# A hybrid attention and mLSTM layer: two loads asked for earlier and an output-gate tile laid across a stage border

## The chip, the cores and the metric

The kernel runs on one core of a Trainium2 chip. The metric is the device time of one execution in microseconds. Before the change it was 2285.49 us, the median of three runs (2283.78 to 2286.15).

The engines are named as in the profile: PE does matrix products and transposes, DVE, ACT and POOL work element by element, SP issues nearly all DMA transfers and does nothing else. Each engine runs its own list of instructions in order and waits on semaphores for the others. An instruction that waits holds up all that stand behind it on its engine.

## The reference

One encoder layer over 2048 positions of width 1024, with batch 1. A conditioning vector gives shifts, scales and gates. Then, in short:

```
hmix = rms_norm(x, g_norm1) * (1 + scale1) + shift1
q_a, k_a, v_a, q_m, k_m, v_m, o_m, gates = split(hmix @ w_in)
att  = rms_norm(banded_attention(q_a, k_a, v_a, sink), g_attn_out)
q_m, k_m = split(silu(centred_dwconv(concat(q_m, k_m))))
h_m  = rms_norm(mlstm(forward) + mlstm(backward), g_mlstm_out)
h_m  = sigmoid(o_m) * h_m
x    = x + gate1 * (concat(att, h_m) @ w_out)
ff   = silu(gte) * up      # gte, up = split(norm2(x) @ w_ffn_in)
x    = x + gate2 * (ff @ w_ffn_out);  out = rms_norm(x, g_final)
```

Attention has 8 heads of 64 with 2 key heads and sees 128 positions to each side. The mLSTM has 4 heads of 128, worked in 16 chunks of 128 positions; each direction carries a state from chunk to chunk. The output gate is the sigmoid of o_m, computed as a tanh.

## The kernel before

**Stages.** The first stage normalises x, keeps its transpose hT on the chip as four blocks of 512 positions, and computes the columns of w_in that are wanted position by position. The second stage (up to about 580 us) computes the mLSTM. The third (to about 800 us) is attention. A tail follows in which the operands of the output projection are made, then the output projection (from 827 us), and from about 1002 us the feed-forward part. The products of the output projection and of the feed-forward part are arranged so that 7 products of half size do the work of 8, so weights are added and subtracted first; w_out's are prepared in stage two (`w_out_ops`) and stored to `wo_d`.

**Filler.** Stages two and three have chains of small work on DVE, ACT and POOL between the products on PE. To keep PE busy, a queue of generators, `fill`, holds the projections of w_in's remaining columns. Each `pull(n)` issues n of their matmuls (128x512, line 498, tile `gps`). A tile of 512 positions is 24 matmuls and a column group of 128 is four such tiles, 96 matmuls. `conv_tile` makes the mLSTM's queries and keys, `qk_att` those of attention, `o_tiles` the output gate (ACT's tanh into `oth`, then a store to `og_d`). A call of `beat` counts one step of a list of things to do later (`put_soon`), so that, say, a store is issued some pulls after its tile. `next_cols` hands out the weights of a column group and starts loading the next group of the list `coming`: a load into the single buffer `wraw`, a rounded copy on ACT (`whi`), and four differences on POOL (`wlo`).

**The backward pass of a head** goes through chunks 15 to 1. For each it transposes the key chunk on PE (line 612, `ktp`), makes a weighted value and a product, and accumulates the state on DVE (line 660, `cb`). Key and value blocks of 512 positions are loaded by `load_qk` and `load_v`, issued on SP in the order of the program. The key and query blocks share four buffers `mqk`. The first query block of the forward pass is asked for at chunk 2:

```
            if cc == 2:
                q_first = load_qk(h, 0, 0)
```

The forward pass multiplies keys and queries (line 679, `sps`), and at the end of each block `store` transposes the scaled result `hst` (line 735, `htp`) and stores it to `mxm_d`.

**Head 0** is prepared while w_out's generator still runs: a loop of 252 steps, one `pull` each, steps w_out's preparation and the gates. The last key block of head 0 is loaded at step 150, the second (`last[NB - 2]`) behind the loop. w_out's last stores are issued at step 242.

**The border.** After the last head the four column groups of attention's keys and first queries are drawn to their end, and then the pools of stage two are closed and those of stage three opened. Up to there the order on all engines is the program's. Behind it, until the tail, PE's order is still the program's, and the order on DVE, ACT, POOL and SP is set by a planner that weighs costs of its own. Stage three loads `skb`, builds the distance bias on POOL and DVE (`iota`, two selections, eight tiles `abias`), and starts with the last query group as its filler, then the output gates of head 0, head 1, and of heads 2 and 3 block by block (`lasts`).

**Attention** goes in 34 steps over 32 units. A step scores one unit (line 782, `as`, tiles `aq`, `ak`, `av` loaded two units ahead), normalises it on POOL (line 798), transposes the unit before (line 805, `atp`) and multiplies the one before that (`ao`). Each step makes ten pulls: one behind each of four scores, one behind the normalisation, one and two and two behind the transposes.

**The tail** loads the prepared w_out (`start_wo`, line 1037) into the buffers of hT blocks that no filler needs any more, splits it on ACT and DVE (`finish_wo`), and draws the rest of `fill`.

Of the kernel before, what the change touches and what calls it, by code (L numbers as in the profile page):

```python
# [21 lines left out]
P = 128  # L22
# [4 lines left out]
NB = T // 512  # L27
# [5 lines left out]
C_QA, C_KA, C_VA, C_QM, C_KM, C_VM, C_OM, C_G = 0, 512, 640, 768, 1280, 1792, 2304, 2816  # L33
# [3 lines left out]
def hybrid_layer_kernel(  # L37
# [14 lines left out]
    def bank(tag, name):  # L52
        return pp.tile([P, 512], F32, tag=tag, name=name, bufs={"g": 2, "a": 2, "b": 1, "c": 2, "d": 1}[tag])
# [55 lines left out]
    fill = deque()  # L109
    soon = []  # L110

    def put_soon(k, f, *args):

        soon.append([k, f, args])

    def beat(k=1):
        for e in soon:
            e[0] -= k
        due = [e for e in soon if e[0] <= 0]
        soon[:] = [e for e in soon if e[0] > 0]  # L120
        for _, f, args in sorted(due, key=lambda e: e[0]):
            f(*args)

    def pull(n=1):

        while n > 0:
            if not fill:
                n -= 1
                beat()
            elif next(fill[0], None) is None:  # L130
                fill.popleft()
            else:
                n -= 1
                beat()

    def finish_fill(g):
        while any(f is g for f in fill):
            pull()
# [102 lines left out]
    def cols_steps(c0):  # L241

        pl, i = wslots[0]
        wslots.rotate(-1)
        r = pl.tile([P, D], F32, tag="wraw", name="wraw", bufs=1)
        v = lambda t: t.rearrange("p (a b) -> p a b", a=KT)
        sp.dma_start(v(r), w_in[:, c0:c0 + P].rearrange("(k p) c -> p k c", p=P))
        yield None
        hi = pl.tile([P, D], F32R, tag=f"w{i}h", name="whi", bufs=1)
        lo = pl.tile([P, D], F32R, tag=f"w{i}l", name="wlo", bufs=1)  # L250
        act.activation(hi, r, AF.Copy)
        for u in range(4):
            q = slice(u * 256, (u + 1) * 256)
            pool.tensor_tensor(lo[:, q], r[:, q], hi[:, q].bitcast(F32), SUB)
            yield v(hi), v(lo)

    def proj_cols(c0):
        *_, w = cols_steps(c0)
        return w

    ready, coming = deque(), deque()

    def next_cols():

        w = ready.popleft()
        if coming and not ready:
            g = cols_steps(coming.popleft())
            put_soon(6, next, g)
            for u in range(3):
                put_soon(40 + 5 * u, next, g)  # L270
            put_soon(55, lambda: ready.append(next(g)))
        return w
# [5 lines left out]
    with tc.tile_pool(name="sw", bufs=2, side="right", reuse_waits="tile") as sw:  # L278
# [29 lines left out]
        def columns_of(z, o, n):  # L308
# [7 lines left out]
                           fill=NEG, base=0, channel_multiplier=-1)  # L316
        pool.affine_select(maskb[:, 1, :], maskb[:, 1, :], pattern=[[-1, P]], compare_op=ALU.is_ge,
                           fill=NEG, base=0, channel_multiplier=1)
# [125 lines left out]
        for n in range(NB):  # L444
# [13 lines left out]
            for i in range(4):  # L458
# [9 lines left out]
                if tt == 8:  # L468
# [3 lines left out]
                    wp = ctx.enter_context(tc.tile_pool(name="w", bufs=1, side="left", reuse_waits="tile"))  # L472
# [22 lines left out]
    def proj_mm(ps, w, n):  # L495
        for k in range(KT):
            for i in range(3):
                pe.matmul(ps, w[i == 2][:, k, :], hT[n](i == 1, k), start=(k == 0 and i == 0),  # L498
                          stop=(k == KT - 1 and i == 2))
                yield True  # L500
# [56 lines left out]
    oslots = deque()  # L557

    def o_tiles(heads, blocks, ws_):

        if not ws_:
            ws_.extend(proj_cols(C_OM + h * P) for h in heads)
        for n in blocks:
            for h, w in zip(heads, ws_):
                ps = bank("g", "gps")
                yield from proj_mm(ps, w, n)
                pl, tag = oslots[0]
                oslots.rotate(-1)
                t = pl.tile([P, 512], F32, tag=tag, name="oth", bufs=1)
                act.activation(t, ps, AF.Tanh, scale=0.5)  # L570
                sp.dma_start(og_d[4 * n:4 * n + 4, h].rearrange("c p t -> p c t"), t.rearrange("p (c t) -> p c t", c=4))

    later = []

    def tick():

        due = [f for k, f in later if k <= 0]
        later[:] = [[k - 1, f] for k, f in later if k > 0]
        for f in due:
            f()  # L580

    def load_v(h, n):
        va = s2.tile([P, 4, 129], F32, tag="mv", name="mv", bufs=2)
        sp.dma_start(va, vaug_d[n * 512:(n + 1) * 512, h, :].rearrange("(c p) d -> p c d", p=P))
        return va

    def load_qk(h, j, n):
        t = s2.tile([P, 512], F32, tag="mqk", name="mqk", bufs=4)
        sp.dma_start(t, qk_d[j, h, n])
        return t  # L590

    def load_last(h):
        return {NB - 1: (load_qk(h, 1, NB - 1), load_v(h, NB - 1))}

    def mlstm(h, nb, nf, last):
# [5 lines left out]
        def load_bc(cc):  # L601
            bc = s2.tile([P, 4, P], F32, tag="bc", name="bc", bufs=3)
            sp.dma_start(bc.rearrange("p j t -> p (j t)"), bc_d[h, cc].rearrange("j t -> (j t)").partition_broadcast(P))
            return bc
# [15 lines left out]
        def kv_mm(kn, vw, tag="a"):  # L620
            kvp = bank(tag, "kvp")
            pe.matmul(kvp[:, :129], kn, vw, start=True, stop=True)
            return kvp
# [17 lines left out]
        for cc in list(range(NT - 1, 0, -1)) + [0, 0, 0]:  # L641
            tick()
            n, i = divmod(cc, 4)
            if i == 3 and n and n - 1 not in blk:
                blk[n - 1] = (load_qk(h, 1, n - 1), load_v(h, n - 1))
            if cc == 2:
                q_first = load_qk(h, 0, 0)
            if cc in (6, 4, 2):
                bcs[3 - cc // 2] = load_bc(3 - cc // 2)
            if cc:  # L650
                todo.append((cc, *k_chunk(blk[n][0][:, i * P:(i + 1) * P], blk[n][1][:, i, :], 1, cc)))
                pull(nb - nb // 2)
            if len(todo) > 2 or (todo and not cc):
                c_, kn, vw = todo.popleft()
                kvp = kv_mm(kn, vw, "bcdc"[c_ % len("bcdc")])
                if c_ == NT - 1:
                    dve.tensor_copy(cb[:, c_ - 1, :], kvp[:, :129])
                else:
                    rr = row(1, c_)
                    dve.scalar_tensor_tensor(cb[:, c_ - 1, :], cb[:, c_, :], dec[:, rr:rr + 1], kvp[:, :129], MUL, ADD)  # L660
                pull(nb // 2)
# [79 lines left out]
        for cc in range(NT + 1):  # L741
            tick()
            if cc == NT - 3 and h + 1 < HM:
                last = load_last(h + 1)
# [227 lines left out]
    ready.extend((w_first, w_second))  # L972
    convs = [[conv_tile(j, h) for j in (1, 0)] for h in range(HM)]
    coming.extend(c0 + h * P for h in range(1, HM) for c0 in (C_KM, C_QM))
    coming.extend(C_QA + j * P for j in (4, 0, 1, 2, 3))
    for h in range(HM):
        fill.extend(convs[h])
    for i in range(2 * 96 + 60):
        for j, g in enumerate(steps):
            while due[j] <= i:  # L980
                due[j] = next(g)
        if i == 150:
            t = s2.tile([P, 512], F32, tag="og", name="mqk", bufs=1)
            sp.dma_start(t, qk_d[1, 0, NB - 1])
            last = {NB - 1: (t, load_v(0, NB - 1))}
        pull(1)
    assert min(due) > 1 << 20
    last[NB - 2] = load_qk(0, 1, NB - 2), load_v(0, NB - 2)
    tags2 = (("cacc", 4), ("ctanh", 2))
    first = [qk_att(s2, tags2, j) for j in (4, 0, 1, 2)]  # L990
    fill.extend(first)
    for h in range(HM):
        if h:
            for g in convs[h]:
                finish_fill(g)
        last = mlstm(h, 3, 11, last)
# [5 lines left out]
    while soon:  # L1002
        beat()
    win.close()
    assert not fill and not later
    s2s.close()
    s3s, mxs = ExitStack(), ExitStack()
    s3 = s3s.enter_context(tc.tile_pool(name="s3", bufs=2, side="right", reuse_waits="tile"))
# [17 lines left out]
    TO = [4 * n + i for n in BO for i in range(4)]  # L1026
    wo23 = []
    lasts = [o_tiles((2, 3), (n,), wo23) for n in BO]
    fill.extend([o_tiles((h,), range(NB), []) for h in (0, 1)] + lasts)
    oslots.append((wp, "oth"))  # L1030
    wo = []

    def start_wo(u):
# [120 lines left out]
    for s_ in range(len(order) + 2):  # L1154
        if s_ + 2 == NT:
            for g in second:
                finish_fill(g)
            beat(1 << 20)
        u0 = None
        if s_ < len(order):  # L1160
            u0 = Unit(*ahead.popleft())
        for g in range(4):
            if u0:
                u0.score(g)
            pull(1)
            if u2 and g < 3:
                u2.values(g)
        if s_ + 2 < len(order):
            ahead.append(att_loads(*order[s_ + 2]))
        if u0:  # L1170
            u0.normalize()
        pull(1)
        for i in range(3):
            if u1:
                u1.transpose(i)
            pull(1 if i == 0 else 2)
        u2, u1 = u1, u0
        if s_ > 20:
            next(chain0, None)
# [772 lines left out]
```

## Time and profile before

| | |
|---|---|
| runs | 2283.78, 2285.49, 2286.15 us |
| profiled execution, span | 2283.0 us (the page gives no other time for it) |
| PE / DVE / ACT / POOL busy | 97% / 71% / 46% / 47% of the span |
| mean granted PE clock | 0.995 |
| DMA | 391.28 MB, mean 171 GB/s |

The span runs from the first instruction to the last; the time of a run has some more around it. In the list of waits a row names the waiting engine, its instruction, the one that released it, and then the microseconds in total, how often, and the longest. In a timeline a row has its start, its length, the engine (SPq for a DMA issue), the line of the kernel, the operation, the tiles, the count, and in brackets the idle time before it and what ended that. Matmuls are pipelined, so the length of one is more than the distance to the next. In the view by windows the columns are the stretch, its length, the busy time of PE, PE's weight loads, DVE, ACT and POOL, the granted clock, the share of DMA and GB/s.

### The profile page before, as it was taken

To read this page: it belongs to the slowest core of one execution; us is meant where nothing else is said; L and a number is where in the kernel's file an instruction comes from. 1 tells how busy PE (TensorE), PEld (TensorE's weight loads), DVE (VectorE), ACT (ScalarE), POOL (GpSimd) and SP (SyncE) were. 2 spreads that over 40 slices of the span, in tenths; PEclk is the share of its full clock that TensorE was granted. 3 is DMA by queue.
4 is the path that set the end of the run, shared out by engine and by line. 5 is a ranking of instruction groups with operands and counts; after the bars stand their busy time and mean duration, and the time that the engine had idled before them with its cause. 6 is when DMAs were issued, how large, how long until landed. Compare 5 with 4: busy or idle time off the path is not lost.

```text
span 2283.0 us, 32447 instructions
## 1 busy us (share of the span) xinstructions
PE 2224.0 (97%) x10822; PEld 1859.5 (81%) x10822; DVE 1610.1 (71%) x2931; ACT 1058.6 (46%) x2206; POOL 1069.3 (47%) x927
## 2 busy tenths in 40 slices
PE   6999999999999999999999999999999999999998
PEld 4997788888788878788888888788888888888887
DVE  6787577656687887786756776666766666785594
ACT  5433565644577755344444444433333333233352
POOL 1006535334333434536656665566666654592020
PEclk9999999999999999999999999999999999999999
DMA  8476755676666576764353453533333374542462
GB/s 331 157 242 213 238 152 172 186 229 191 194 179 186 177 234 218 267 221 134 111 171 111 152 180 134 178 108 108 100 106 103 105 255 147 162 155 93 140 220 92
DMA packets 352811, 391.28 MB, mean 171 GB/s; under 512 B 21260, under 2 KB 251004, under 8 KB 352644
## 3 DMA queue, kind: packets, MB, share of 16 engines
q1 hardware_dynamic: 352420, 389.18, 52.5%
q8 instruction: 85, 1.39, 0.2%
q14 instruction: 82, 0.67, 0.1%
q10 hardware_dynamic: 224, 0.04, 0.0%
HBM read 269.95 MB, written 119.19 MB: 170 GB/s over the span
## 4 chain that ended last, share of the span: by engine, by line
PE 51%; DVE 3%; DMA 1%; issue 1%; ACT 1%; POOL 1%; SPq 0%; ACTq 0%; POOLq 0%; DVEq 0%
PE fp L56 11%; PE fp L57 11%; PE fp L58 11%; PE fo L58 5%; PE fo L57 5%; PE fo L56 5%; PE ops L56 1%; PE ops L57 1%; DMA al<-a_d 1%; PE ops L58 1%; DVE w L1721 1%; DVE al L1712 1%; DVE ra L1851 1%; PE trn L183 0%; DMA T<-hop_d 0%
## 5 line engine op out<-in xcount | busy, mean ns | idle before, releaser
L498 PE MATMUL gps<-hT,whi 128*128 128x512 f32 x1088 | 397.3, 420 | 0.3 <-DVE cacc L513 0.3
L57 PE MATMUL fo<-w,ah 128*128 128x512 f32 x616 | 239.8, 389 | 1.1 <-DVE w L1721 1.1
L58 PE MATMUL fo<-w,al 128*128 128x512 f32 x616 | 239.8, 389 | 0.5 <-DVE al L1712 0.5
L56 PE MATMUL fo<-w,ah 128*128 128x512 f32 x616 | 239.7, 389 | 0.0
L498 PE MATMUL gps<-hT,wlo 128*128 128x512 f32 x544 | 226.9, 417 | 0.0
L498 PEld LDWEIGHTS gps<-hT,whi 128*128 128x128 f32 x1088 | 200.5, 191 | 24.5 <-DVE cacc L513 0.7
L56 PE MATMUL fp<-T,S 128*128 128x512 f32 x528 | 206.9, 392 | 1.9 <-ACT s L1608 1.9
L57 PE MATMUL fp<-T,S 128*128 128x512 f32 x528 | 205.6, 389 | 0.0
L58 PE MATMUL fp<-T,S 128*128 128x512 f32 x528 | 205.4, 389 | 0.0
L1712 DVE TENSOR_TENSOR al<-al,ah 128x1024 fp32r<-128x1024 f32 x77 | 119.3, 1552 | 109.2 <-ACT ah L1711 109.0
L1711 ACT ACTIVATE ah<-al 128x1024 fp32r<-128x1024 f32 x77 | 81.6, 1060 | 188.5 <-DMA al<-a_d 186.9
L1451 DVE TENSOR_TENSOR S<-sf,S 128x512 fp32r<-128x512 f32 x86 | 130.4, 1554 | 37.4 <-ACT S L1450 37.2
L1451 DVE TENSOR_TENSOR A<-graw,A 128x512 fp32r<-128x512 f32 x86 | 128.4, 1515 | 16.3 <-ACT A L1450 16.3
L58 PE MATMUL fp<-B,A 128*128 128x512 f32 x352 | 136.9, 389 | 0.0
L56 PE MATMUL fp<-B,A 128*128 128x512 f32 x352 | 136.9, 389 | 0.0
L57 PE MATMUL fp<-B,A 128*128 128x512 f32 x352 | 136.9, 389 | 0.0
L57 PEld LDWEIGHTS fo<-w,ah 128*128 128x128 f32 x616 | 115.6, 188 | 25.6 <-DVE w L1721 1.6
L58 PEld LDWEIGHTS fo<-w,al 128*128 128x128 f32 x616 | 115.6, 188 | 24.9 <-DVE al L1712 1.0
L56 PEld LDWEIGHTS fo<-w,ah 128*128 128x128 f32 x616 | 115.6, 188 | 24.3 <-ACT ah L1711 0.2
L1616 DVE SCALAR_TENSOR_TENSOR g<-t,g 128x512 f32<-128x512 f32 x44 | 41.3, 939 | 132.2 <-ACT t L1615 132.2
L1455 POOL TENSOR_TENSOR sf<-A,A22r 128x512 f32<-128x512 f32 x43 | 61.0, 1419 | 154.9 <-DMA A22r<-in_w_ffn_in_dram 130.8
L798 POOL TENSOR_SCALAR ap<-ap,adn 128x384 f32<-128x384 f32 (+1 forms) x128 | 73.0, 590 | 129.2 <-DVE adn L796 71.7
(418 smaller groups left out, 6166.8 us busy)
## 6 DMA issues: line engine op xcount, KB each, us to landing
al<-a_d SPq DMA_DIRECT2D x77, 512.0 KB, 3.8
wmod<-in_w_mod_dram SPq DMA_DIRECT2D x48, 512.0 KB, 7.3
graw<-in_w_ffn_in_dram SPq DMA_DIRECT2D x43, 512.0 KB, 4.0
a_d<-ka SPq DMA_DIRECT2D x66, 256.0 KB, 4.6
bc<-bc_d SPq DMA_DIRECT2D x64, 256.0 KB, 3.7
hop_d<-n SPq DMA_DIRECT2D x56, 256.0 KB, 4.5
a_d<-u SPq DMA_DIRECT2D x55, 256.0 KB, 4.8
mqk<-qk_d SPq DMA_DIRECT2D x44, 256.0 KB, 4.0
```

What stands on the lines that cost most here:

```text
L56: pe.matmul(o, lh, rh, start=first, stop=False, skip_group_check=skip)
L57: pe.matmul(o, lh, rl, start=False, stop=False, skip_group_check=skip)
L58: pe.matmul(o, ll, rh, start=False, stop=last, skip_group_check=skip)
L498: pe.matmul(ps, w[i == 2][:, k, :], hT[n](i == 1, k), start=(k == 0 and i == 0), stop=(k == KT - 1 and i == 2))
L798: pool.tensor_scalar(self.p[g][:, :self.NK], self.p[g][:, :self.NK], dn[:, g:g + 1], 0.0, MUL, ADD)
L1451: dve.tensor_tensor(t[:, 1, :], f, t[:, 0, :].bitcast(F32), SUB)
L1455: pool.tensor_tensor(f1, a21, a22, ADD)
L1616: dve.scalar_tensor_tensor(g0, t0, 1.0, g0, ADD, MUL)
L1711: act.activation(ah, al.bitcast(F32), AF.Copy)
L1712: dve.tensor_tensor(al, al.bitcast(F32), ah.bitcast(F32), SUB)
L1721: dve.tensor_tensor(w[:, 1, :], f, w[:, 0, :].bitcast(F32), SUB)
L1851: dve.tensor_tensor(ra[i], ra[i], xr, ADD)
```

## The change

Three things are changed.

1. In each backward pass the first query block is asked for at chunk 6.
2. The second key block of head 0 and its values are asked for at step 222 of the loop, so their loads stand on SP ahead of w_out's last six stores.
3. The output gate of head 0 becomes a filler of its own, `o_first`, at the end of stage two's queue. Its weights are handed out by `next_cols`, so those of the last query group are loaded behind them. It is begun in stage two and finished in stage three. In exchange one pull is left out in every second step of attention.

```
-            if cc == 2:
+            if cc == 6:
                 q_first = load_qk(h, 0, 0)
...
-    coming.extend(C_QA + j * P for j in (4, 0, 1, 2, 3))
+    coming.extend(C_QA + j * P for j in (4, 0, 1, 2))
+    coming.extend((C_OM, C_QA + 3 * P))
...
+        if i == 222:
+            last[NB - 2] = load_qk(0, 1, NB - 2), load_v(0, NB - 2)
         pull(1)
     assert min(due) > 1 << 20
-    last[NB - 2] = load_qk(0, 1, NB - 2), load_v(0, NB - 2)
...
     fill.extend(first)
+
+    def o_first():
+        yield from o_tiles((0,), range(NB), [next_cols()])
+
+    fill.append(o_first())
+    oslots.append((wp, "oth"))
...
-    assert not fill and not later
+    assert len(fill) == 1 and not later
...
-    fill.extend([o_tiles((h,), range(NB), []) for h in (0, 1)] + lasts)
-    oslots.append((wp, "oth"))
+    fill.extend([o_tiles((1,), range(NB), [])] + lasts)
...
-            pull(1 if i == 0 else 2)
+            pull(1 if i == 0 or i == 2 and s_ % 2 else 2)
```

## The prediction

> **What bounds the kernel now.** I read the page's busy shares first, then the list of waits for PE, then the timeline around each wait that the change touches.
>
> ```profile
> PE 2224.0 (97%) x10822; PEld 1859.5 (81%) x10822; DVE 1610.1 (71%) x2931; ACT 1058.6 (46%) x2206; POOL 1069.3 (47%) x927
> ```
>
> PE is busy 97% of the 2283.0 us span, so only its idle time (59 us) and its pace can change. The list of waits says which idle time this change aims at (total, times, longest):
>
> ```profile
> PE htp L735 <- POOL hst L730: 5.6, 1, 5.6
> PE sps L679 <- DMA mqk<-qk_d: 3.2, 2, 1.7
> ...
> PE ktp L612 <- DMA mqk<-qk_d: 2.0, 1, 2.0
> ...
> PE sps L679 <- DVE cb L660: 1.1, 1, 1.1
> ```
>
> The first is the border between the mLSTM stage and the attention stage, the second the first query block of two heads, the third the second key block of head 0. The border costs more than its wait. The view by windows gives the granted clock in its sixth column of numbers, the timeline the pace:
>
> ```profile
> 574.20:579.60 5.40, 0.00 (x0) 0.00 (x0) 3.87 (x15) 1.34 (x6) 3.46 (x6) 0.91 0.41 103
> 579.60:585.30 5.70, 5.63 (x16) 4.57 (x17) 1.19 (x3) 0.69 (x1) 1.43 (x4) 0.50 0.62 198
> ```
>
> ```profile
> 579.67 1.12 PE L735 MATMUL htp<-ident,hst 128*128 128x128 f32 x4 [5.64 <-POOL hst L730]
> 580.44 1.20 PE L498 MATMUL gps<-hT,whi 128*128 128x512 f32 x2
> ...
> 588.10 0.39 PE L498 MATMUL gps<-hT,wlo 128*128 128x512 f32 x1
> 588.33 0.62 PE L498 MATMUL gps<-hT,whi 128*128 128x512 f32 x2
> 588.78 0.39 PE L498 MATMUL gps<-hT,wlo 128*128 128x512 f32 x1
> ...
> 591.06 0.28 PE L782 MATMUL as<-ak,aq 128*128 128x256 f32 x1
> ```
>
> Three matmuls take 0.68 us at full clock (588.10 to 588.78), 0.227 each. After 5.4 us without a matmul the clock is 0.50 for 5.7 us: the 36 matmuls from 580.44 to 591.06 take 10.6 us where 36 x 0.227 = 8.2, and the four transposes take 0.77 instead of some 0.45. So the border costs 5.6 + 2.4 + 0.3 = 8.3 us.
>
> **The change part by part.** (A) Query block at backward chunk 6 instead of 2. No instruction is added; one 256 KB load moves past two loads of bc and one or two stores on SP.
>
> ```profile
> 337.74 0.40 SPq L584 DMA_DIRECT2D mv<-vaug_d  x1
> ...
> 340.23 0.60 SPq L589 DMA_DIRECT2D mqk<-qk_d  x1
> ```
>
> ```profile
> 346.13 0.46 PE L679 MATMUL sps<-mqk 128*128 128x128 f32 x2 [1.50 <-DMA mqk<-qk_d]
> ```
>
> In head 1 it now goes out right behind the value load, near 338.2, 2.0 us earlier, so it lands 2.0 us before 346.1; PE needs it at 344.6. The wait of 1.5 goes, with 0.5 to spare; in the other head (longest 1.7) it goes too. Late next is DVE's cb, whose banks the same product needs: the list's 1.1 us is that wait, in head 0. I leave 0.3 per head for it and take a gain of 2.6 (ends: 0 where cb is just as late, 3.2). The bc loads behind it go out 0.5 us later; they are wanted only at the end of the backward pass. Its buffer was last read six chunks before, so SP does not wait.
>
> (B) Second key block of head 0 at step 222, ahead of w_out's last six stores.
>
> ```profile
> 249.32 0.30 PE L612 MATMUL ktp<-ident,mqk 128*128 128x128 f32 x1 [1.95 <-DMA mqk<-qk_d]
> ```
>
> ```profile
> 241.51 0.32 SPq L122 DMA_DIRECT2D qk_d<-cacc  x1
> ...
> 245.52 0.45 SPq L589 DMA_DIRECT2D mqk<-qk_d  x1
> ```
>
> In the new order of SP the load and its value load stand right behind the 241.51 store: 3.6 us earlier, so it lands near 245.7 and PE wants it at 247.4. The six stores go 1 us later; nothing reads them before the output projection. Gain 1.9 (ends 0 and 1.95).
>
> (C) The output-gate tile across the border. By the order of PE's instructions 34 filler matmuls (7.7 us) leave the later stages and stand before the first attention score: 17 taken from the attention loop (the shorter pull in every odd step), 17 from the tail behind it. The last state product is 3 matmuls later than before, then come 6 matmuls, 4 transposes and 20 matmuls, 5.9 us in all, ahead of the last transposes. The chain that they wait for took from 573.2 to 579.6 in the old trace, 6.4 us from the same product, partly because DVE's small steps shared that time with POOL's weight split, which the new order has behind it. I take no wait there (0 to 0.5). With full clock the first score would come at 591.06 - 8.3 + 7.7 = 590.4.
>
> But the order adds a wait behind it. POOL now has the four splits of the next query weights between the last hst and the iota of the attention bias, and SP has the load of another weight tile, which needs the buffer that those splits read, ahead of skb and of the first aq, ak and av.
>
> ```profile
> 572.74 1.06 ACT L251 ACTIVATE whi<-wraw 128x1024 fp32r<-128x1024 f32 x1 [2.51 <-PE gps L498]
> ...
> 581.75 0.69 ACT L737 ACTIVATE og<-htp,gml 128x512 f32<-128x512 f32 x1 [5.72 <-DMA mxm_d<-og]
> ```
>
> ```profile
> 573.87 2.77 POOL L254 TENSOR_TENSOR wlo<-wraw,whi 128x256 fp32r<-128x256 f32 x4 [4.62 <-ACT whi L251]
> ```
>
> ```profile
> 582.92 0.45 SPq L1012 DMA_DIRECT2D skb<-in_sink_dram  x1
> 583.42 0.47 SPq L762 DMA_DIRECT2D aq<-qst_d  x1
> 583.94 0.50 SPq L764 DMA_DIRECT2D ak<-kst_d  x1
> ```
>
> ```profile
> ak<-kst_d SPq DMA_DIRECT2D x4, 256.0 KB, 3.3
> ```
>
> On ACT the split's first half follows og, which ends near 582.1 as now; 1.06 makes 583.1, the four POOL splits 2.77 make 585.9, the weight load 0.45 and skb 0.45 put aq at 587.0 and ak at 587.5 instead of 583.94. With 3.3 us to landing and, as my estimate, 0.6 for the 512 KB in front, ak is there at 591.4 to 591.6, against 590.4: a new wait of 1.2 us (ends 0, and 5 if the weight load is slow). The bias on DVE, behind POOL's iota, is ready near 590.5 by the same sum, just in time. So the score comes at 591.6, 0.5 later than now.
>
> The attention loop is PE's:
>
> ```profile
> 592.00:790.00 198.00, 195.73 (x1084) 168.41 (x1082) 157.94 (x462) 156.46 (x419) 80.32 (x141) 0.99 0.64 192
> ```
>
> 195.7 of 198 us busy, DVE 80%, ACT 79%. 17 matmuls less are 3.9 us. The planner also gives DVE another order there: most units now have all their value splits ahead of the scores, where before many had one between the sum and the reciprocal of the softmax, which makes POOL's normalisation late. I take 0.5 of the 2.2 us of small waits. Gain 4.4 (ends 0 and 6).
>
> The tail is different. There the 17 matmuls less only bring PE earlier to a point that is set by loads:
>
> ```profile
> 821.89 1.06 ACT L1041 ACTIVATE wo<-wo 128x1024 fp32r<-128x1024 f32 x1 [2.69 <-DMA wo<-wo_d]
> ...
> 826.80 0.58 ACT L570 ACTIVATE oth<-gps 128x512 f32<-128x512 f32 x1
> ```
>
> ```profile
> 827.43 0.50 PE L56 MATMUL ops<-wo,mA 128*128 128x512 f32 x1
> ```
>
> The first product of the output projection needs the bank that ACT's oth at 826.80 empties, and that stands on ACT behind six splits of wo, each waiting for its load. These loads follow, on SP, the last store of attention, which does not come earlier relative to the loop's end. Only one og_d store (now ahead) leaves the queue. I take 0.8 of the 3.9 us (ends 0 and 3.9); the other 3.1 become a new wait at ops, behind ACT's oth.
>
> Sum: -2.6 - 1.9 + 0.5 - 4.4 - 0.8 = -9.2, taken as **-9.0**. The profiled execution's span is 2283.0; the runs' median is 2285.49, 2.5 above it, which I keep: 2276.5.
>
> The row on the clock bears on both new waits: 5.4 us idle cost half the clock, the 1.95 us at 249.32 none (matmuls go on at full pace). By the Trainium skill (TensorE: Matmul & The Clock Gate, Part 1) the clock falls to half after an idle window of about 3.4 us, and the window runs free. By that page the tail's 3.1 us may or may not be hit; the sum would be 2.4 us smaller by the border's row if it is.
>
> **Rivals.**
> (R1) The tail is not bound by ACT: the wo loads come early enough and PE keeps all 3.9. For it: DMA engines are not full there in every slice. Against: the 2.69 us for which ACT waits. Time: 2276.5 - 3.1 = 2273.4.
> (R2) The border's wait takes the place of the one removed: ak or the bias comes 5 us late, the clock halves again, 5 + 2.4 + 0.3 = 7.7 instead of 1.2. For it: og, whi, wlo, weight load and aq are one chain through four queues. Against: 3.3 us to landing. Time: 2276.5 + 6.5 = 2283.
> (R3) Slower: attention becomes bound by normalisation.
>
> ```profile
> 619.34 2.27 POOL L798 TENSOR_SCALAR ap<-ap,adn 128x384 f32<-128x384 f32 x4 [5.60 <-DVE adn L796]
> ```
>
> ```profile
> 622.00 0.38 PE L805 MATMUL atp<-ident,ap 128*128 128x128 f32 x2
> ```
>
> POOL ends at 621.61, 0.39 before PE uses it. If the new order makes DVE's part later so that each of 32 units waits 0.6 us, 19 us come back: 2295.7. It decides from 0.43 us a unit ((9.0 + 4.6) / 32). Against: the new DVE order looks better, not worse.
> (R4) A and B do nothing, since cb and bc are as late as the loads: 2276.5 + 4.5 = 2281.0.
>
> **How the numbers follow.** Forecast 0.54, R1 0.12, R2 0.13, R3 0.13, R4 0.08. A measurement tells this kernel from no change at about 0.2%, 4.6 us. Faster by more: forecast and R1, 0.66, and half of R4, 0.70; within: R2 and half of R4, 0.17; slower: R3, 0.13. The range 2271 to 2285 leaves out R3 and a little of R1's far end (every end at its best gives 2285.5 - 3.2 - 1.95 - 0.7 - 6 - 3.9 = 2269.7); at the top it takes in R2. The likeliest case alone is 2273 to 2280.
>
> **What would show it.** Right: no htp wait on hst, no ktp wait on mqk, sps waits of at most 0.6 us for mqk, clock 1.00 between the last state product and the first score, a wait of about 1 us of the first score on ak, and about 3 us of the first ops product on ACT's oth. Wrong: a clock of 0.5 after the first score or after the tail's wait, an ap wait on abias, or many atp waits on POOL.

## The result and the profile after

The changed kernel takes 2281.54 us (median of 15 runs, 2278.15 to 2282.63); beside it, the kernel before took 2285.49 us (15 runs, 2282.77 to 2289.8). The ratio is 0.998, with a 95% interval of 0.9973 to 0.9987. The kernel is faster by 0.2%, some 4 to 4.6 us, which is half of the 9.0 us that were forecast. The profiled execution has a span of 2279.7 us.

The list of waits for PE in the changed kernel between 240 and 1003 us (total, times, longest):

```profile
PE ops L56 <- ACT oth L570: 3.4, 1, 3.4
PE aps L1127 <- POOL msq L1079: 2.2, 3, 0.8
PE as L782 <- DMA ak<-kst_d: 2.0, 1, 2.0
PE ao L818 <- DVE aptl L142: 1.7, 6, 0.7
PE ops L56 <- DVE xr L1225: 1.4, 2, 0.9
PE kvp L622 <- ACT vw L617: 1.4, 2, 1.2
PE sps L679 <- DVE cb L660: 1.1, 1, 1.1
```

The 5.6 us of htp on hst, the 3.2 of sps on mqk and the 2.0 of ktp on mqk are gone. Three waits are new: ops on ACT's oth, as on ak, and kvp on ACT's vw. The timeline of PE has one row for each, and kvp's comes where the query block used to be awaited:

```profile
343.85 0.49 PE L622 MATMUL kvp<-vw,kn 128*128 128x129 f32 x2 [1.18 <-ACT vw L617]
...
587.47 0.36 PE L782 MATMUL as<-ak,aq 128*128 128x256 f32 x1 [2.02 <-DMA ak<-kst_d]
...
821.75 0.51 PE L56 MATMUL ops<-wo,mA 128*128 128x512 f32 x1 [3.45 <-ACT oth L570]
```

The view by windows of the changed kernel, around the waits of as and of ops (the granted clock is the sixth number behind the stretch's length, just ahead of the DMA share):

```profile
584.00:587.40 3.40, 1.45 (x7) 0.87 (x5) 1.32 (x6) 0.00 (x0) 0.00 (x0) 1.00 0.98 262
587.40:591.20 3.80, 3.73 (x14) 3.28 (x15) 2.07 (x9) 1.90 (x7) 0.00 (x0) 0.55 1.08 326
591.20:595.00 3.80, 3.80 (x20) 3.31 (x19) 2.32 (x10) 2.52 (x9) 1.21 (x3) 1.00 0.62 169
818.50:821.70 3.20, 0.00 (x0) 0.00 (x0) 3.20 (x4) 2.76 (x5) 0.00 (x0) 1.00 1.03 357
821.70:823.90 2.20, 2.15 (x10) 1.87 (x11) 2.20 (x3) 2.20 (x5) 0.00 (x0) 0.86 0.53 153
823.90:826.60 2.70, 2.70 (x8) 2.15 (x8) 2.70 (x6) 1.40 (x3) 1.66 (x2) 0.50 0.67 181
```

Soon behind each of these two waits the clock is halved for 3.4 us.

Spans of single executions differ by a few microseconds for reasons that have nothing to do with the change, so I compare stages. The table gives the time between five points, each the start of one matmul in PE's timeline: the first key-value product and the first score of head 0, the first attention score, the values product just ahead of the last unit's fourth score, near the end of the attention loop (called the mark), and the first product of the FFN on T and S. The mark before and after:

```profile
789.98 0.50 PE L818 MATMUL ao<-aptl,av 128*128 128x512 f32 x1 [0.63 <-DVE aptl L142]
```

```profile
785.19 0.39 PE L818 MATMUL ao<-aptl,av 128*128 128x512 f32 x1
```

| us | kvp to score | score to attention | attention to mark | mark to FFN | FFN to end |
|---|---|---|---|---|---|
| before | 17.14 | 328.20 | 198.92 | 217.90 | 1275.2 |
| after | 15.11 | 327.87 | 197.72 | 217.13 | 1277.4 |
| difference | -2.03 | -0.33 | -1.20 | -0.77 | +2.2 |

I take the last column for no effect of the change: in the fourteen profiled executions of this study, one of each kernel, the FFN took 1275.2 to 1279.9 us, and the one shown of the kernel before is the shortest of all. The stretch ahead of the first point (245.72 us before, 244.49 after) is left out too; in the fourteen it took 241.9 to 247.5. From the first point to the FFN the change is worth 4.3 us.

### The profile page after: what moved, and what is told of

The parts are those of the page before. It is cut to its first block, busy times and chain, and to the rows that moved or that the text cites. A ratio compares the mean times of both kernels' runs of the same rounds, so it can differ in the third digit from the quotient of the medians.

```text
span 2279.7 us, 32432 instructions
## 1 busy us (share of the span) xinstructions
PE 2225.9 (98%) x10822; PEld 1858.6 (82%) x10822; DVE 1610.1 (71%) x2931; ACT 1059.1 (46%) x2206; POOL 1067.4 (47%) x927
## 4 chain that ended last, share of the span: by engine, by line
PE 51%; DVE 3%; DMA 2%; issue 1%; ACT 1%; POOL 1%; SPq 0%; ACTq 0%; DVEq 0%; POOLq 0%
PE fp L56 11%; PE fp L57 11%; PE fp L58 11%; PE fo L58 5%; PE fo L57 5%; PE fo L56 5%; PE ops L56 1%; DMA al<-a_d 1%; PE ops L58 1%; PE ops L57 1%; DVE ra L1858 1%; DVE w L1728 0%; DVE al L1719 0%; PE trn L183 0%; DMA B<-hop_d 0%
```

## The experiments

**The parts alone.** Three kernels: the query block at chunk 6 and nothing else (A); the second key block at step 222 and nothing else (B); the change without either (C).

```
a_only, against before          b_only, against before
-            if cc == 2:        +        if i == 222:
+            if cc == 6:        +            last[NB - 2] = load_qk(0, 1, NB - 2), ...
...
c_only, against the changed kernel
-            if cc == 6:
+            if cc == 2:
...
-        if i == 222:
-            last[NB - 2] = load_qk(0, 1, NB - 2), load_v(0, NB - 2)
         pull(1)
     assert min(due) > 1 << 20
+    last[NB - 2] = load_qk(0, 1, NB - 2), load_v(0, NB - 2)
```

> The kernel before with the query block asked for at chunk 6 and nothing else. Theory 1 (the terms were right in kind, wrong in size): the two waits of sps on mqk (3.2 us) go, and a wait of about 1.2 us of kvp on ACT's vw comes in head 1, so that some 1.4 us are left: 2284.1 us, and no sps wait on mqk in the trace but the one of the second key block's kind. Theory 2 (the forecast gain of this part and the next was never there, all of the measured gain comes from the border): 2285.5 us, with other waits of the same sum in place of the 3.2 us.

> The kernel before with the second key block of head 0 asked for at step 222, ahead of w_out's last stores, and nothing else. Theory 1: the wait of ktp or kvp at 249 us (1.95 us) goes and nothing takes its place: 2283.6 us, first score of head 0 earlier by 1.9 us against its own stage border. Theory 2: the wait is only moved to the next DMA of the queue: 2285.5 us.

> The change without its two moved loads: only the output-gate tile across the border and the 17 pulls cut from the attention loop. Theory 1: at the border 8.3 us go, 7.7 us of fillers come and a wait of some 2 us on ak with some 1.9 us of halved clock behind it; the loop gives 4.4 us; in the tail 3.9 us of fillers go and a wait of 3.4 us with some 1.4 us of halved clock comes; sum about -0.2 us: 2285.3 us. Theory 2 (the border and the loop carry the whole gain): 2281.5 us.

Measured: A 2283.78 us, ratio 0.9991 (0.998 to 1.0002); B 2282.15 us, 0.9997 (0.9986 to 1.0007); C 2284.19 us, 0.9997 (0.9988 to 1.0006), the kernel before 2284.23 us beside them. The runs can't tell any of the three from no change. The stages can:

| us | kvp to score | score to attention | attention to mark | mark to FFN |
|---|---|---|---|---|
| before | 17.14 | 328.20 | 198.92 | 217.90 |
| A alone | 18.93 | 326.05 | 200.18 | 217.47 |
| B alone | 15.20 | 328.19 | 197.72 | 217.39 |
| C alone | 16.98 | 329.95 | 197.74 | 216.49 |

A takes 2.1 us out of the second column, B 1.9 out of the first, C puts 1.75 into the second and takes 1.2 out of the third and 1.4 out of the fourth. So theory 2, by which A and B do nothing, falls. The third column has to be read with care: A and B leave the attention loop as it is, and it took 200.18 and 197.72 us there against 198.92. In the kernel before and in A alone the clock is halved for 3.4 us in the loop (from 728.78 and 728.28 us), in B alone it is not. A does bring its own wait: in the timeline of A alone stands

```profile
348.68 0.49 PE L622 MATMUL kvp<-vw,kn 128*128 128x129 f32 x2 [1.19 <-ACT vw L617]
```

where ACT stood at the decay rows of the next chunk (a wait of 1.54 us on POOL's ng in the changed kernel). It was there before, behind PE's wait for the query block.

**All 34 matmuls out of the loop.**

```
-            pull(1 if i == 0 or i == 2 and s_ % 2 else 2)
+            pull(1 if i == 0 or i == 2 else 2)
```

> The changed kernel with the second pull of i == 2 cut in every step of the attention loop, so that 34 matmuls come out of the loop in place of 17, and the tail after it has as many fillers as the kernel before had. Theory 1: the tail's wait (3.4 us) and the halved clock behind it (about 1.4 us) go, its 17 fillers come back (3.9 us), and the loop gives another 3.9 us: 4.8 us faster than the changed kernel, 2276.7 us, no wait of ops on ACT oth over 0.5 us, clock 1.00 around the first ops. Rival (with two pulls fewer in a step the loop is held by DVE and POOL): the loop gives nothing more, 2280.6 us, with waits of as, ao or atp longer by some 4 us in sum.

Measured: 2280.82 us, ratio 0.9984 (0.9975 to 0.9993), what the rival gave. Attention to mark took 200.00 us, 2.3 more than with 17 cut, and the timelines of PE and ACT say where:

```profile
785.69 0.80 PE L817 MATMUL ao<-apth,av 128*128 128x512 f32 x1 [3.38 <-ACT apth L141]
826.21 0.50 PE L56 MATMUL ops<-wo,mA 128*128 128x512 f32 x1 [0.42 <-ACT oth L570]
```

```profile
781.45 1.06 ACT L1048 ACTIVATE wo<-wo 128x1024 fp32r<-128x1024 f32 x1 [3.11 <-DMA wo<-wo_d]
```

The tail's wait did go (0.42), but near the end of the loop, behind the first of the last unit's scores, PE waits 3.38 us for ACT. ACT had stood 3.11 us at a split of wo whose load had not landed, and what PE waited for stood behind that in ACT's queue. In the changed kernel the two splits of wo that stand in the loop's end (769.52 us) wait for nothing. So the time is the rival's, but the loop was held at one place by a late load and not by DVE or POOL, and this run does not show what 34 matmuls fewer are worth without that wait.

**The waits filled with idle matmuls.** Does the halved clock cost what its matmuls lose?

```
+    def idle_mm(n):
+        ps = bank("d", "dum")
+        for i in range(n):
+            pe.matmul(ps, hT[3](0, 0, slice(0, 128)), hT[3](0, 0), start=True, stop=True)
...
     pull(36)
+    idle_mm(9)
...
+    idle_mm(15)
     start_wo(6)
```

> The changed kernel with matmuls whose result nobody reads put into its two new waits: 9 (about 2.0 us) ahead of the first score, 15 (about 3.4 us) ahead of the first output product. The work of the kernel and its waits stay as they are. Theory 1 (behind each wait the clock is halved for 3 to 4 us because TensorE had been idle): both stretches run at clock 1.00, first as and first ops start as before, and what comes behind them is 1.9 and 1.4 us earlier: 3.2 us faster than the changed kernel, 2278.3 us. Rival (the slow stretches come of the DMA traffic, whose share is 0.9 to 1.05 there, and not of the idle time): the matmuls there still take 0.42 us a piece, 2281.5 us.

Measured: 2281.54 us, ratio 0.9982 (0.9973 to 0.9992) to 2285.52 us: no gain over the changed kernel's 0.998. The windows show that the mechanism is right:

```profile
588.40:592.10 3.70, 3.70 (x20) 3.25 (x21) 2.00 (x9) 1.67 (x7) 0.00 (x0) 1.00 1.14 343
592.10:596.00 3.90, 3.38 (x15) 2.15 (x14) 2.67 (x11) 3.13 (x11) 1.74 (x4) 1.00 1.12 345
822.00:824.00 2.00, 2.00 (x12) 1.71 (x12) 2.00 (x2) 2.00 (x5) 0.00 (x0) 1.00 0.51 148
824.00:826.70 2.70, 2.70 (x14) 2.15 (x13) 2.70 (x6) 1.39 (x3) 1.75 (x1) 1.00 0.86 255
```

The clock stays at 1.00 with a DMA share much like the changed kernel's (0.5 to 1.1), so the slow stretches come of idle time and not of the traffic. But theory 1 missed the time, and the rival has the time without its mechanism: attention to mark took 197.29 us (0.4 less than after), mark to FFN 216.80 (0.3 less). Part of what the faster matmuls win is waited for again a few microseconds on: 0.52 us of idle time in the second row above, and in the output projection 0.68 us here

```profile
828.93 0.47 PE L56 MATMUL ops<-wo,mS 128*128 128x512 f32 x1 [0.68 <-ACT mA L1116]
```

and 0.36 us at 838.18, of which the changed kernel has neither.

**The attention loads ahead of the weight load.**

```
-            ws_.extend(proj_cols(C_OM + h * P) for h in heads)
+            with tc.issue_after(av_load[1]) if heads == (1,) else ExitStack():
+                ws_.extend(proj_cols(C_OM + h * P) for h in heads)
```

av_load holds the value loads of the attention units, so the weight load stays behind the first two units' loads on SP.

> The changed kernel with the load of the second output-gate columns (wraw) queued on SP behind the first two attention loads in place of ahead of them. Theory 1 (ak is late because SP stands at wraw until POOL has split the columns before it, 580.7 us): ak is asked for some 4 us earlier, the wait of as on ak (2.0 us) and the halved clock behind it (1.9 us) go: 3.9 us faster than the changed kernel, 2277.6 us. Rival (the next thing is late: the bias tiles on DVE, or aq, which has to wait for the last qst_d stores): the first score still starts some 2 us after the last filler, 2281.5 us.

Measured: 2279.12 us, ratio 0.9972 (0.9962 to 0.9981) to 2285.52 us. SP's timeline, of the changed kernel and then of this one:

```profile
576.91 0.36 SPq L122 DMA_DIRECT2D mxm_d<-og  x1
580.76 0.37 SPq L247 DMA_DIRECT2D wraw<-in_w_in_dram  x1
581.22 0.53 SPq L1020 DMA_DIRECT2D skb<-in_sink_dram  x1
581.81 0.43 SPq L762 DMA_DIRECT2D aq<-qst_d  x1
582.29 0.50 SPq L764 DMA_DIRECT2D ak<-kst_d  x1
```

```profile
577.97 0.37 SPq L122 DMA_DIRECT2D mxm_d<-og  x1
578.43 0.46 SPq L1022 DMA_DIRECT2D skb<-in_sink_dram  x1
578.98 0.42 SPq L763 DMA_DIRECT2D aq<-qst_d  x1
579.49 0.46 SPq L765 DMA_DIRECT2D ak<-kst_d  x1
...
584.75 1.61 SPq L247 DMA_DIRECT2D wraw<-in_w_in_dram  x1
```

In the changed kernel SP stands 3.5 us at wraw, until POOL has split the tile that lay in its buffer, at 577.91 + 2.82 = 580.73:

```profile
577.91 2.82 POOL L254 TENSOR_TENSOR wlo<-wraw,whi 128x256 fp32r<-128x256 f32 x4 [3.43 <-ACT whi L251]
```
With ak asked for 1.5 us behind og's store instead of 5.4, no wait of as is left, and the clock stays up:

```profile
586.30:590.10 3.80, 3.80 (x22) 3.32 (x22) 1.99 (x10) 2.73 (x10) 0.00 (x0) 1.00 1.09 325
```

Score to attention took 325.32 us (2.5 less than after), attention to mark 196.17 (1.6 less). Theory 1 holds at its place. Of the 3.9 us expected at the end, 1.8 are seen by the two kernels' ratios and 2.5 by their distances from the median beside them.

**The tail's order.** Three orders were tried, each alone and together with the border's mend. The first puts the splits of wo 2 behind the loads of wo 4 and 5, and those of wo 5 behind the next output-gate tile.

```
-    finish_wo(2)
     finish_fill(lasts[2])
     for u in (4, 5):
         start_wo(u)
+    finish_wo(2)
...
-    finish_wo(5)
     pull(26)
+    finish_wo(5)
```

> The changed kernel with another order in the tail: the splits of wo 2 are queued behind the output-gate tiles of block 2 and the loads of wo 4 and 5, and the splits of wo 5 behind the next output-gate tile. Theory 1 (the first output product waits for a PSUM bank, whose tanh stands on ACT behind wo copies, which wait for loads that SP issued late behind a store of oth): the wait of ops on ACT oth (3.4 us) and the halved clock behind it (1.4 us) go: up to 4.8 us faster than the changed kernel, 2276.7 us. Rival (the loads are held by the DMA engines, busy share 1.0 from 800 to 823 us, and not by the order): the wait stays over 2.5 us, 2281 us.

> The border of one and the tail of the other together. Theory 1: the gains add, 8.7 us faster than the changed kernel at most, 2272.8 us, without a wait of PE over 1.5 us between 300 and 1000 us. Rival: what the border gains is lost as wait in the tail, whose loads start from the end of the attention loop and are held by the DMA engines: 2277 us.

The second also puts two of the mS operands ahead of wo 4:

```
     finish_wo(3)
-    finish_wo(4)
     pull(26)
-    finish_wo(5)
     for _ in range(2):
         nxt.both()
+    finish_wo(4)
     while fill:
         pull()
+    finish_wo(5)
```

> The changed kernel with the tail's splits in the order in which the products need them: the loads of wo 4 and 5 ahead of the splits of wo 2, two of the mS operands ahead of the splits of wo 4, and wo 5 behind the last output-gate tile. Same instructions, other order on ACT, DVE and SP. Theory 1b (the tail is set by DVE's queue, where eight splits of wo, 9.2 us in one row, stand ahead of the mS operands; fillers taken out of PE there are worth nothing): first ops at about 818.2 us as in the other tail order, but without its wait of 4.0 us on mA, so that the FFN starts some 3.6 us earlier than in the changed kernel: 2277.9 us. Rival (DVE, ACT and the DMA engines are all full there, and any order ends at the same time): waits of ops on ACT or DVE of together 3 to 4 us come back at some other product, 2281.5 us.

> The same tail order together with the attention loads queued ahead of the second output-gate columns. Theory 1b: the border's gain, 2.3 us at the first score and about 1.3 us of clock in the loop, reaches the end together with the tail's 3.6 us: 2275 us, with no PE wait over 1.5 us between 300 and 1000 us. Rival (the tail takes back what the border gains): 2279 us, as with the border alone.

The third takes the splits of wo 5 and the last two mS operands behind the first product of the output projection:

```
-    finish_wo(5)
     start_wo(6)
-    for _ in range(2):
-        nxt.both()
...
             if p == 0:
+                if i in (4, 5):
+                    cur.both()
+                if i == 6:
+                    finish_wo(5)
```

> The tail order of the run before, and behind it the splits of wo 5 and the last two mS operands moved from ahead of the output projection to behind its first product, so that DVE's queue has the first addition into xr (which frees the PSUM bank that the third product adds to) ahead of them. Theory 1c (the third product waited for that addition, 0.7 us of work behind 9 us of DVE queue, and not for ACT): the wait of 3.9 us at the third product falls under 1.5 us, the FFN starts some 4 us earlier than with the order of the run before: 2277 us. Rival (DVE has the same work in all and the wait comes back at the fifth or sixth product): 2280.5 us.

> The same with the attention loads ahead of the second output-gate columns. Theory 1c: 2274 us (the border's 3 us beside the tail's). Rival: 2278.5 us.

| | median us | ratio, interval | mark to FFN us | largest PE wait there |
|---|---|---|---|---|
| after | 2281.54 | 0.998 (0.9973 to 0.9987) | 217.13 | 3.45 at the first product |
| first order | 2283.0 | 0.9984 (0.9973 to 0.9995) | 218.06 | 3.97 at the third |
| second | 2280.54 | 0.998 (0.9971 to 0.9989) | 217.84 | 3.92 at the third |
| third | 2282.76 | 0.9983 (0.9974 to 0.9993) | 217.73 | 3.49 at a later one |
| border | 2279.12 | 0.9972 (0.9962 to 0.9981) | 217.01 | 2.34 at the first |
| border, first | 2278.29 | 0.997 (0.9959 to 0.998) | 218.28 | 4.28 at the third |
| border, second | 2278.63 | 0.9976 (0.9967 to 0.9986) | 217.51 | 3.89 at the third |
| border, third | 2277.87 | 0.996 (0.9947 to 0.9972) | 217.35 | 3.50 at a later one |

In each of the six the time came out within 2.3 us of the rival's: the wait changed its place and the stretch did not get shorter. In the timelines of the first, second and third order alone, the wait stands here:

```profile
828.38 0.77 PE L56 MATMUL ops<-wo,mS 128*128 128x512 f32 x1 [3.97 <-ACT mA L1116]
```

```profile
825.80 0.77 PE L56 MATMUL ops<-wo,mS 128*128 128x512 f32 x1 [3.92 <-ACT mA L1116]
```

```profile
832.67 0.77 PE L56 MATMUL ops<-wo,mS 128*128 128x512 f32 x1 [3.49 <-DVE xr L1225]
```

The releaser ACT, inferred by the profile, is not the cause in the first two. With border and second order together DVE's timeline has, around the same product (823.42 us there),

```profile
815.27 4.63 DVE L1051 TENSOR_TENSOR wo<-wo 128x1024 fp32r<-128x1024 f32 x4
819.82 0.69 DVE L1122 TENSOR_TENSOR mS<-ma,mS 128x512 fp32r<-128x512 f32 x1
820.42 0.69 DVE L1122 TENSOR_TENSOR mS<-mm,mS 128x512 fp32r<-128x512 f32 x1
821.02 1.65 DVE L1096 SCALAR_TENSOR_TENSOR ma<-ma,cols,arb 128x256 f32<-128x256 f32 x4
822.59 0.69 DVE L1227 TENSOR_TENSOR xr<-xr,ops 128x512 f32<-128x512 f32 x1
```

and the third product adds into the bank that the last of these reads, 0.7 us of work behind 7.3 us of queue (815.27 to 822.59). With the first order alone it is the same, an addition into xr from 827.55 to 828.23 behind a queue that is full from 815.63 us. So in these orders DVE's queue sets when the wait ends. In the changed kernel DVE is the fullest engine from the end of the loop on:

```profile
799.00:824.00 25.00, 21.45 (x99) 17.33 (x97) 22.51 (x35) 16.34 (x22) 9.95 (x8) 0.99 0.98 324
```

22.5 of 25 us for DVE, 21.5 for PE, and the DMA engines at 0.98. That DVE alone sets the stretch was not shown, since no run took work away from it. What is shown is that PE's matmul count hardly does: mark to FFN is 216.5 to 218.3 us in all fourteen executions. It is 217.4 to 217.9 in the three with the tail's fillers as before, and 216.5 to 217.1 in the three with 19 matmuls (4.3 us) fewer there and the splits in the old order (after, C alone, border). It is 216.50 with all 34 taken from the loop, where the fillers are back, and 216.80 with 15 matmuls added. The first product stands anywhere from 33.0 to 38.3 us behind the mark.

The kernel with the border's mend beats the kernel before. Against the changed kernel its interval overlaps (0.9962 to 0.9981, 0.9973 to 0.9987); for a gain speak the 4.1 us in the two stages, and that all four kernels with this mend have a lower ratio than every kernel without it. The intervals of the versions with another tail beside it overlap with its own.

## Why the prediction was right or wrong

The time is 5.0 us above the forecast and inside the range, but outside the 2273 to 2280 us of the likeliest case. A gain beyond 4.6 us was given 0.70. What came is faster clear of the noise, but with 4.0 us by the medians and 4.6 by the ratio it lies at or below that border. It is also the time of R4 (2281.0), whose mechanism did not come, so the time alone says little. Step by step, in stages of the profiled executions:

- **A, forecast -2.6: right in kind, 2.1 to 2.5 measured** (328.20 to 326.05 alone; from C alone, 329.95, to a mean of 327.5 in the six kernels with the whole change and the old border). Late next was not DVE's cb but ACT's vw in head 1, for which I had left 0.3.
- **B, -1.9: right.** 17.14 to 15.11 us, and 15.20 alone.
- **C at the border, +0.5: +1.4 to +1.75 measured** (from A alone, 326.05, to the same 327.5; C alone). The old wait and its cold clock went as forecast: the matmuls run through from the last state product to the first score. The new wait stood where I had put it, behind wraw on SP, but took 2.02 us instead of 1.2. I had the load's landing at 3.3 + 0.6 us; issued at 582.29 and used at 587.47, it took some 5.1. No run shows the 0.6, and the 3.3 was the wrong row: only one of those four loads has a landing on record, and it was issued at 680.46 us, while the load of ak issued at 585.51, at the old border itself, landed after 5.0.
- **The attention loop, -4.4: -1.2 measured. This is the step that failed most.** I priced 17 matmuls at their whole 3.9 us, from a loop at full clock, with 0.5 of small waits on top. In the changed kernel the loop begins with 3.4 us at half clock, because of the wait just ahead of it, and I priced that wait without its clock, although I had the clock's price for the old border in hand. Where the wait is gone (border) the loop gives 2.7. That leaves 1.7 of the 4.4. Two of the 17 matmuls (0.45) stand behind the mark, and the 0.5 of small waits did not come: PE's waits between the first score and the mark rose from 1.56 to 2.45 us, aptl's alone in the list from 0.9 to 1.7. How much of the loop's time really is PE's stays open, since the three executions with the loop uncut took 197.72 to 200.18 us there. Each of these figures is good to about 1 us.
- **The tail, -0.8: right, -0.8 measured.** 3.4 us of wait came for the matmuls that went, at ops on ACT's oth, against 3.1 forecast. The three executions with the tail's fillers as before spread over 0.5 us, so the agreement to a tenth is luck.

The sum by these terms is about -2.3 - 1.9 + 1.6 - 1.2 - 0.8 = -4.6, where the stages gave -4.3. Of the 4.6 us that are missing against the sum of -9.2, 3.2 went in the loop, 1.1 at the border and 0.3 in A.

Two readings in the working are off by some 0.4 us and change nothing in this: by the row shown ACT's og ends at 582.44 and not near 582.1, and 26 matmuls with four transposes are 6.4 us by the prices given there and not 5.9.

Of the signs I had named, all the right ones are there (no htp wait, no ktp wait on mqk, clock 1.00 up to the first score, waits of ops and as), and so are two of the wrong ones: a clock of 0.5 behind the first score and behind the tail's wait. Of the rivals, R2 came about in part: ak late and the clock halved, with 2 us in the place of 5. R1 (all 3.9 us of the tail) and R3 (POOL's normalisation) did not; R4 fell with A and B.

The price of the clock itself also has to be read with care. 3.8 us at a clock of 0.55 lose 1.7 us of matmul pace, yet filling the wait with idle matmuls gave back 0.4 in the loop. PE's waits up to the mark were 0.5 us longer there; why the rest did not come is not shown. Bringing the load forward gave 2.5 us at the score and 1.6 in the loop.

## What to carry to other kernels

When a moved block of fillers lets PE arrive earlier at a point, look for who sets that point: where the stretch is held by another engine's queue, fillers taken out of it are worth little (here some 0.8 us for 4.3 us of matmuls), and a reordering only moves the wait. A load behind another load that waits for its buffer is late by that buffer's whole chain, so ask of each queue what its head waits for, and put the load that PE needs first ahead of it. And price a new wait of 2 us with the clock behind it, but only up to the next wait that would have come anyway.

## What the runs showed of the hardware

I had not expected the clock to halve after waits this short, nor so irregularly. In the granted clock behind single waits of PE: 1.33 us halved it (kernel before, in the attention loop, which I had taken to be at full clock), 1.60 did not (all 34 cut), 1.83 did (C alone), 1.88 did not (third order), 1.95 did not (before, at ktp), 2.02 did (after), 2.17 did (A alone, whose first column above is 1.8 us longer). And the same wait at the same product, 3.49 us in the third order alone and 3.50 with the border's mend, halved the clock in one and not in the other.

The clock's own records order this. In all fourteen traces, behind the first 60 us and ahead of the last 10, the clock is halved for 3.41 or 6.83 us and nothing else, and within a trace all these stretches begin a whole number of 3.413 us apart. So the time can be cut into pieces of 3.413 us at these borders. Of the 19 pieces at full clock in which PE was busy for under 1.6 us, 18 were followed by a halved clock; the nineteenth, with 1.59 us, holds the wait of 1.95 us at ktp. Of over 9000 others two were (1.85 and 1.87 us busy, at the same place of the attention loop in the kernel before and in A alone; why is not shown). So the halving goes by PE's busy time in such a piece and not by the length of a wait, and a wait that a border cuts in two can leave enough on both sides. In the views of the changed kernel, of the third order alone and of the third order with the border's mend the first number behind the stretch's length is PE's busy time:

```profile
584.38:587.79 3.41, 1.39 (x8) 0.91 (x7) 0.94 (x4) 0.00 (x0) 0.00 (x0) 1.00 1.03 282
587.79:591.20 3.41, 3.41 (x14) 2.93 (x13) 2.07 (x9) 1.90 (x7) 0.00 (x0) 0.50 1.08 329
```

```profile
827.96:831.37 3.41, 1.22 (x6) 0.68 (x4) 3.10 (x15) 0.00 (x0) 0.00 (x0) 1.00 0.00 0
831.37:834.79 3.42, 2.12 (x5) 1.76 (x6) 2.69 (x6) 0.63 (x1) 0.99 (x1) 0.50 0.01 2
```

```profile
827.39:830.80 3.41, 1.69 (x8) 1.07 (x6) 3.17 (x13) 0.00 (x0) 0.00 (x0) 1.00 0.00 0
830.80:834.22 3.42, 1.65 (x7) 1.42 (x8) 2.65 (x7) 0.62 (x1) 0.53 (x1) 1.00 0.00 0
834.22:837.63 3.41, 2.69 (x12) 1.93 (x12) 3.37 (x3) 1.57 (x4) 3.33 (x3) 1.00 0.55 154
```

The Trainium skill (TensorE: Matmul & The Clock Gate, Part 1) says that the window in which idle time is watched runs free. The even borders agree with that. Its length there, 3413 ns, is that of the pieces; but if the window has to be idle throughout, 17 of the 20 pieces do not fit, in which PE was busy for 0.09 to 1.87 us, and here the measurement decides.
